# Value products of prompt attention: four key blocks at a time instead of two, with nine exponential buffers instead of six

## The chip, the core and the metric

One NeuronCore of a Trainium2 chip runs the whole program. The time is device microseconds (us) of one execution; the median of three runs is compared. In the profile PE is TensorE (matmuls), PEld its weight loads, DVE is VectorE, ACT is ScalarE, POOL is GpSimd and SP the engine that issues most DMAs.

## What is computed

One inference step of a decoder layer, for a prompt of 1024 tokens and for 8 single tokens with a cache of 1024 positions each: RMS norm, one input projection, then two mixers side by side (sparse attention and a gated delta rule), an output projection, a SwiGLU feed-forward part and a last norm. The change lies in the sparse attention of the prompt, which the reference computes for blocks of 128 queries:

```python
p_cmp = masked_softmax(einsum('bqgrd,bngd->bqgrn', qf, ck), m_cmp)      # 63 compressed keys
o_cmp = einsum('bqgrn,bngd->bqgrd', p_cmp, cv)
s_sel = einsum('bqgrd,bgqkld->bqgrkl', qf, kg)                          # selected key blocks
o_sel = einsum('bgqrkl,bgqkld->bqgrd', masked_softmax(s_sel, m_sel), vg)
p_win = masked_softmax(einsum('bqgrd,bsgd->bqgrs', qf, kw), m_win)      # last 512 keys
o_win = einsum('bqgrs,bsgd->bqgrd', p_win, vw)
return g[..., 0:1] * o_cmp + g[..., 1:2] * o_sel + g[..., 2:3] * o_win
```

There are 8 query heads in 2 groups of 4, each head 64 wide, and one key/value head for a group. All is float32.

## The kernel before, in words

A *unit* is one block of 128 queries (i = 0 to 7) with one head group (g = 0 or 1), 16 in all, in the order of UNITS (L911): i = 2, 1, 0, 5, 4, 3, 7, 6, both groups of each. For a unit the scores are computed twice. `score_maxima` (L1014) puts queries on partitions and finds each row's maximum (DVE, L1049) and sum of exponentials (ACT, L1051), in banks of PSUM named S (three of them); its products are L1044 and L1045. `offset_rows` (L1056) turns them into one additive offset per query and branch, which also holds the gate and the softmax's denominator, and writes it into rows of the tile qo. `values_unit` (L1111) then computes the scores again with keys on partitions: for each block of keys two products (L1131, L1132) into one of two banks named X, an exponential on ACT into a buffer PF (L1134), which is the weighted probability at once, and on some blocks a mask on DVE (L1137). With the offset in place the outputs of the three branches can simply be added up, so all value products of a unit (`weighted`, L1124) accumulate into one bank, O.

A unit's blocks are numbered n = 0 to N-1: n = 0 is the block of 63 compressed keys (64 rows), then come i + 1 blocks of 128 selected keys and up to 5 of the window. N is 3, 5, 7, 9, 11, 12, 13, 14 for i = 0 to 7, so 74 blocks per group and 148 in all. A value product has 64 output columns, half of TensorE's width: an even n writes partitions 0 to 63 of O, an odd one 64 to 127, and `write_unit` (L1151) adds the halves and stores them. The list `late` holds blocks whose value product is not yet issued. Whenever it holds four, the two oldest are taken out and issued, the odd one first; at the unit's end the rest follows in pairs, each after a `yield`. `keep_in_program_order` pins a product behind the PE instruction that was issued before it in the program.

Several streams of work share the engines. `schedule` (L134) interleaves them by a virtual clock: each generator yields its cost and a pause, and the first of the streams whose pause is over goes on. The streams are the rest of the input projection, `small_streams` (L884), and for attention one each for queries, maxima, offsets, values and `attention_post`. small_streams goes through the delta rule, then the attention of the 8 single tokens (`sample_attention`, which gathers cached keys by indirect DMAs into gx, L1309, copies them by DMA into cpx and kx, L1314 and L1315, and multiplies by `compress`, L812), the residual (L1480), and the output projection of the first two thirds of the tokens (`out_proj`, L1530, six matmuls between two yields). Within what the streams put out, the program's builder orders each engine's instructions again by its own estimate of when their data is there.

The steps below are at L1122 to L1126 (`weighted`), L1133 (the buffers), L1138 (when products are due) and L1143 to L1147 (the unit's end).

Of the kernel before, what the change touches and what calls it, by code (L numbers as in the profile page):

```python
# [9 lines left out]
F32 = mybir.dt.float32  # L10
# [74 lines left out]
def hybrid_step(ctx, tc, A, O):  # L85
# [37 lines left out]
    def bank(tag="mm"):  # L123
        tag = ALIAS.get(tag, tag) if tag not in ps_bufs else tag
        if tag == "g":
            return psg.tile([128, 512], F32, name="g", bufs=2)
        return ps_now[0].tile([128, 512], F32, name=tag, bufs=ps_bufs[tag])
# [806 lines left out]
    def attention_values(start, done):  # L934
        for u, (i, g) in enumerate(UNITS):
            yield lambda: done["F"] > u and done["P"] >= u - 0
            start["o", u] = yield from values_unit(start["aw"], start["stack", g], start[u], g, i, start["keep"])
            done["C"] += 1
# [71 lines left out]
    def window(i):  # L1010
        w0 = 128 * max(0, i - 4)
        return 128 * (i + 1), w0, 128 * (i + 1) - w0
# [98 lines left out]
    def values_unit(aw, st, q, g, i, keep):  # L1111
        nk, w0, nw_ = window(i)
        md, mw, mc = keep[:, 0:128], keep[:, 128:256], keep[:64, 256 + 128 * i:384 + 128 * i]
        qt, qo = q
        blocks = [(0, "c", 0, 64, mc)]
        blocks += [(1, "s", 128 * k, 128, md if k == i else None) for k in range(i + 1)]
        blocks += [(2, "w", 128 * k, 128, md if k == i else mw if k == i - 4 else None)
                   for k in range(w0 // 128, i + 1)]
        O = bank("O")
        last = len(blocks) - 1  # L1120

        def weighted(due):  # L1122
            for n, pf, v, w in reversed(due):
                x = mm(O[64 * (n % 2):64 * (n % 2) + 64], lhsT=v, rhs=pf[:w], start=n < 2, stop=n > last - 2)  # L1124
                if n != due[-1][0]:
                    tc.keep_in_program_order(x)  # L1126

        late = []
        for n, (br, nm, a, w, mask) in enumerate(blocks):
            p = bank("X")  # L1130
            mm(p[:w], lhsT=st[nm + "h"][:, a:a + w], rhs=qt, start=True, stop=False)  # L1131
            mm(p[:w], lhsT=st[nm + "l"][:, a:a + w], rhs=qo, start=False, stop=True)  # L1132
            pf = aw.tile([128, 512], F32, name="PF", bufs=6)  # L1133
            S.activation(pf[:w], p[:w], AF.Exp)  # L1134
            if mask is not None:
                pv = pf[:w].rearrange("p (h t) -> p h t", h=4)
                V.tensor_tensor(pv, pv, mask[:, None, :].to_broadcast([w, 4, 128]), op=OP.min)  # L1137
            due = late[:2] if len(late) == 4 else []  # L1138
            del late[:len(due)]
            weighted(due)  # L1140
            late.append((n, pf, st[nm + "v"][:w, a // 128], w))
            yield 0.43 + 0.43 * len(due), 0.4 * (n < 3)
        while late:  # L1143
            due = late[:2]
            del late[:2]
            yield 0.0, 0.5
            weighted(due)  # L1147
        yield 0.87, 1.0
        return O
# [502 lines left out]
    def pair_tiles(gw, ht, u, slots=range(7)):  # L1652
        if u % 2 == 0:
            return [gw.tile([128, 2, 512], F32R, name=f"q{x}") for x in slots]
        a = ht.tile([128, 4, 2, 512], F32R, name="hTa")
        b = ht.tile([128, 3, 2, 512], F32R, name="hTb")
        return [a[:, x] for x in range(4)] + [b[:, x] for x in range(3)]
# [85 lines left out]
    def pair_blocks(raws):  # L1743
        return [r[:, :, 128 * x:128 * x + 128] for x in range(2) for r in raws]
# [253 lines left out]
    with tail, pool("hn") as hp, pool("gw") as gw:  # L1998
# [3 lines left out]
        with pool("psc", space=PSUM) as ps:  # L2002
# [93 lines left out]
            w, a = pair_tiles(gw, None, 0, range(4)), pair_blocks(raws)  # L2096
# [11 lines left out]
        with pool("psd", space=PSUM) as ps:  # L2108
# [11 lines left out]
            for u in range(20):  # L2120
# [17 lines left out]
                w = w_next  # L2138
            keep.flush()
        with pool("psf", space=PSUM) as ps:  # L2140
# [4 lines left out]
            for v in range(20):  # L2145
# [36 lines left out]
                w = w_next  # L2182
# [29 lines left out]
```

## Time and profile before

| | |
|---|---|
| median of three runs | 1788.6 us (1788.4 to 1796.88) |
| the profiled execution | 1790.07 us |
| its span, first to last instruction | 1788.4 us |
| PE busy | 1689.1 us, 94% of the span |
| DVE, ACT, POOL busy | 1123.1, 832.6, 400.5 us |
| first and last start of an L1124 record | 546.9 and 1033.6 us |

Busy time is the union of an engine's instructions, not their sum, and a matmul's record reaches to its modelled end, so consecutive matmuls overlap in the records: what one costs is read from start to start. A product in float32 has two records. In the timeline view, consecutive records of the same form are put in one row, with their count.

### The profile page before, as it was taken

What the parts mean: (1) busy time and instruction counts of PE and PEld (TensorE: products, weight loads), DVE (VectorE), ACT (ScalarE), POOL (GpSimd) and SP (SyncE); (2) the same over time, 40 slices, a digit from 0 to 9 for tenths busy, and PEclk for the clock granted to TensorE, in tenths of its full rate; (3) what the DMA queues carried; (4) which work ended last, traced back from release to release, by engine and by line L of the source; (5) the groups of instructions that cost most, each with busy time, mean ns of one, the idle gap of its engine ahead of it and who ended that gap; (6) DMA issues with size and microseconds to landing.
All of it is one profiled execution on the core that took longest, in us unless ns stands there. A gap on an engine that the chain in (4) does not pass through costs nothing.

```text
span 1788.4 us, 32029 instructions
## 1 busy us (share of the span) xinstructions
PE 1689.1 (94%) x11985; PEld 1502.5 (84%) x11985; DVE 1123.1 (63%) x2841; ACT 832.6 (47%) x1986; POOL 400.5 (22%) x405
## 2 busy tenths in 40 slices
PE   7999989989989989989999989999999999999998
PEld 7999989989876465555567769999999999999997
DVE  6458874588468766656754377544444444868786
ACT  5567742222356656646864454433333333633222
POOL 1214330222112221110023453332332334100000
PEclk9999999999989889899999999999999999999999
DMA  7135444665331475552444342233222323533212
GB/s 237 41 103 193 177 157 132 213 214 178 103 103 36 129 211 143 161 158 75 148 117 138 117 134 63 97 102 111 84 84 83 97 82 108 178 126 124 96 59 95
DMA packets 247584, 223.81 MB, mean 125 GB/s; under 512 B 76121, under 2 KB 226145, under 8 KB 245246
## 3 DMA queue, kind: packets, MB, share of 16 engines
q1 hardware_dynamic: 232404, 188.79, 34.2%
q0 software_dynamic: 7152, 22.43, 3.9%
q10 hardware_dynamic: 7874, 10.56, 1.8%
q8 instruction: 94, 1.54, 0.3%
q14 instruction: 60, 0.49, 0.1%
HBM read 149.08 MB, written 60.40 MB: 117 GB/s over the span
## 4 chain that ended last, share of the span: by engine, by line
PE 58%; DVE 4%; DMA 4%; ACT 4%; issue 2%; POOL 1%; SPq 0%; POOLq 0%; ACTq 0%; DVEq 0%
PE X L1763 13%; PE Z L1937 6%; PE V L1763 6%; PE Z L1919 5%; PE O L1124 4%; PE g L1530 4%; PE Y L1763 3%; PE mm L1455 2%; DMA gx<-in_cache_nsa_kv_dram,ix 2%; PE S L1044 2%; PE X L1131 2%; PE S L1045 1%; PE Y L1979 1%; PE X L371 1%; PE X L1132 1%
## 5 line engine op out<-in xcount | busy, mean ns | idle before, releaser
L77 DVE TENSOR_TENSOR q<-q,q 128x256 fp32r<-128x256 f32 (+5 forms) x234 | 139.2, 610 | 50.5 <-ACT q L77 49.0
L77 ACT CAST q<-q 128x256 fp32r<-128x256 f32 (+2 forms) x195 | 90.3, 495 | 129.2 <-DVE q L77 79.2
L1051 ACT ACTIVATE S<-S,nb 128x512 f32<-128x512 f32 (+4 forms) x256 | 119.8, 469 | 47.3 <-DVE nb L1049 39.9
L1049 DVE TENSOR_REDUCE nb<-S 128x1 f32<-128x512 f32 (+4 forms) x154 | 96.2, 636 | 14.7 <-PE S L1045 13.3
L1134 ACT ACTIVATE PF<-X 128x512 f32<-128x512 f32 (+1 forms) x148 | 84.9, 595 | 43.6 <-PE X L1132 38.0
L287 PE MATMUL X<-xh,ch_h 128*128 128x344 f32 x288 | 95.0, 330 | 0.0
L371 PE MATMUL X<-wh,xh 128*128 128x320 f32 (+1 forms) x288 | 93.6, 325 | 0.0
L77 DVE TENSOR_TENSOR q<-q,Y 128x258 f32<-128x258 f32 x40 | 16.9, 424 | 121.4 <-PE Y L1763 85.2
L77 ACT COPY q<-X 128x258 f32<-128x258 f32 x80 | 30.0, 375 | 135.5 <-PE X L1763 135.5
L287 PE MATMUL X<-xl,ch_h 128*128 128x344 f32 x288 | 92.7, 322 | 0.0
L287 PE MATMUL X<-xh,ch_l 128*128 128x344 f32 x288 | 92.7, 323 | 0.0
L371 PE MATMUL X<-wh,xl 128*128 128x320 f32 (+1 forms) x288 | 91.3, 317 | 0.1
L371 PE MATMUL X<-wl,xh 128*128 128x320 f32 (+1 forms) x288 | 91.2, 317 | 0.1
L1722 POOL TENSOR_TENSOR q<-q,q 128x512 f32<-128x512 f32 x40 | 58.8, 1470 | 135.2 <-DVE q L77 107.4
L1497 POOL TENSOR_TENSOR wol<-woraw,woh 128x1024 fp32r<-128x1024 f32 x18 | 43.7, 2434 | 88.5 <-ACT woh L1496 88.5
L1137 DVE TENSOR_TENSOR PF<-PF,keep 128x512 f32<-128x512 f32 (+1 forms) x56 | 40.3, 725 | 30.5 <-ACT PF L1134 30.2
L77 POOL TENSOR_TENSOR q<-q,q 128x258 f32<-128x258 f32 (+1 forms) x44 | 46.5, 1068 | 48.9 <-DVE q L77 48.9
L1124 PE MATMUL O<-PF,vs 128*64 128x512 f32 x144 | 54.5, 647 | 1.5 <-DVE o L1155 1.5
L287 PEld LDWEIGHTS X<-xh,ch_h 128*128 128x128 f32 x288 | 54.9, 191 | 0.2 <-ACT craw L245 0.2
L252 DVE SCALAR_TENSOR_TENSOR cacc<-craw,stt,cacc 128x1024 f32<-128x1024 f32 x36 | 53.1, 1475 | 3.0 <-ACT cacc L250 2.7
L287 PEld LDWEIGHTS X<-xl,ch_h 128*128 128x128 f32 x288 | 54.8, 190 | 0.1
L371 PEld LDWEIGHTS X<-wl,xh 128*128 128x128 f32 x288 | 54.4, 189 | 0.4 <-DVE wl L350 0.4
(758 smaller groups left out, 5582.6 us busy)
## 6 DMA issues: line engine op xcount, KB each, us to landing
q<-in_w_gate_up_dram SPq DMA_DIRECT2D x40, 512.0 KB
woraw<-in_w_out_dram SPq DMA_DIRECT2D x23, 512.0 KB
q<-g_scr SPq DMA_DIRECT2D x22, 516.0 KB
q<-in_w_down_dram SPq DMA_DIRECT2D x22, 512.0 KB
g_scr<-q SPq DMA_DIRECT2D x40, 258.0 KB
k_scr<-pack SPq DMA_DIRECT2D x8, 1280.0 KB
packr<-k_scr SPq DMA_DIRECT2D x8, 1280.0 KB
cpx<-gx SPq DMA_DIRECT2D x64, 128.0 KB
```

Source lines behind the costliest of these rows:

```text
L77: i = op(*args, **kw)
L287: mm(p[:, :CH], lhsT=a[:, k], rhs=b[:, k, CH * c:CH * c + CH], start=k == 0 and j == 0, stop=k == 7 and j == 2)
L371: mm(p[:, :ncol], lhsT=a[:, k, c0:c0 + 128], rhs=b[k][:, :ncol], start=k == 0 and j == 0, stop=k == 7 and j == 2)
L1049: V.tensor_reduce(out=nb[:, y, br, h0:h0 + per], in_=pv, op=OP.max, axis=AX.X, negate=True)
L1051: S.activation(pv[:, h], pv[:, h], AF.Exp, bias=nb[:, y, br, h0 + h:h0 + h + 1], accum_out=sm[:, y, br, h0 + h:h0 + h + 1])
L1124: x = mm(O[64 * (n % 2):64 * (n % 2) + 64], lhsT=v, rhs=pf[:w], start=n < 2, stop=n > last - 2)
L1134: S.activation(pf[:w], p[:w], AF.Exp)
L1530: mm(p[:, :n], lhsT=x[:, k], rhs=y[:, :n], start=i == 0 and j == 0, stop=i == 7 and j == 2)
L1722: plan.setdefault(step, []).append(lambda: eng.tensor_tensor(out, x, y, op=op))
L1763: mm(p, lhsT=w[n][:, x, c], rhs=y[:, k, 258 * q:258 * q + 258], start=new and k == 0 and j == 0, stop=k == nk - 1 and j == 2, skip_group_c ...
L1919: mm(p[:, q], lhsT=w[2 * x + k2][:, y, c], rhs=b[:, k, 258 * q:258 * q + 258], start=k2 == 0 and k == 0 and j == 0, stop=k2 == 1 and k == ...
L1937: mm(p[:, q], lhsT=w[n][:, x, c], rhs=y[:, k, 258 * q:258 * q + 258], start=new and k == 0 and j == 0, stop=k == 1 and j == 2, skip_group_ ...
```

## The change

The buffers PF become nine. Value products are issued when `late` holds six blocks, and then the four oldest; the rest at a unit's end goes in groups of four as well. Within a group the order is pair by pair, the odd block of each first: 1, 0, 3, 2. All but the first of a group are pinned. The cost that the stream reports grows with the group.

```diff
         def weighted(due):
-            for n, pf, v, w in reversed(due):
+            order = [d for k in range(0, len(due), 2) for d in due[k:k + 2][::-1]]
+            for n, pf, v, w in order:
                 x = mm(O[64 * (n % 2):64 * (n % 2) + 64], lhsT=v, rhs=pf[:w], start=n < 2, stop=n > last - 2)
-                if n != due[-1][0]:
+                if n != order[0][0]:
                     tc.keep_in_program_order(x)
...
-            pf = aw.tile([128, 512], F32, name="PF", bufs=6)
+            pf = aw.tile([128, 512], F32, name="PF", bufs=9)
...
-            due = late[:2] if len(late) == 4 else []
+            due = late[:4] if len(late) == 6 else []
             del late[:len(due)]
             weighted(due)
...
         while late:
-            due = late[:2]
-            del late[:2]
+            due = late[:4]
+            del late[:4]
             yield 0.0, 0.5
             weighted(due)
```

## Rows read from the trace of the kernel before

**Rows 1.** The head of the page: span, and PE's and PEld's busy time.

```profile
span 1788.4 us, 32029 instructions
PE 1689.1 (94%) x11985; PEld 1502.5 (84%) x11985; DVE 1123.1 (63%) x2841; ACT 832.6 (47%) x1986; POOL 400.5 (22%) x405
```

**Rows 2.** Windows view of the attention stage: stretch, length, then busy time of each engine.

```profile
620.00:690.00 70.00, 58.63 (x335) 40.42 (x334) 46.88 (x131) 45.57 (x140) 14.70 (x21) 0.93 0.73 206
...
740.00:800.00 60.00, 51.59 (x277) 32.56 (x279) 36.73 (x102) 34.86 (x91) 10.63 (x17) 0.94 0.65 179
800.00:1035.00 235.00, 222.99 (x1212) 150.80 (x1209) 127.31 (x305) 140.53 (x346) 53.81 (x37) 0.98 0.37 116
```

**Rows 3.** The same windows for L1124 alone: PE busy, PEld busy.

```profile
547.00:620.00 73.00, 24.58 (x52) 4.33 (x52) 0.93 0.31 83
...
800.00:1035.00 235.00, 51.59 (x158) 9.44 (x154) 0.98 0.37 116
sum 488.00, PE 109.20 PEld 19.79; mean PE 21.84 PEld 3.96
```

**Rows 4.** Chain of waits by line, in 620 to 690, 740 to 800, 800 to 1035 us.

```profile
by line: DMA gx<-in_cache_nsa_kv_dram,ix 21.5%; DMA kx<-gx 18.9%; PE O L1124 7.0%; SPq L1314 6.9%; issue 6.5%; PE S L1044 4.7%; PE S L1045 4.0%; PE g L835 3.9%; DVE nb L1049 3.7%; ACT kt L838 3.1%; ACT S L1051 3.0%; PE g L1330 2.6%; PE g L1
...
by line: DMA gx<-in_cache_nsa_kv_dram,ix 35.3%; DMA kx<-gx 11.6%; issue 6.5%; PE O L1124 5.9%; PE X L1131 5.8%; DVE nb L1049 5.1%; PE X L1132 4.2%; PE g L1321 3.0%; PE g L835 2.9%; DVE S L1048 2.6%; PE S L1044 2.0%; DVE PF L1137 2.0%; DVE o
...
by line: PE g L1530 29.1%; PE O L1124 16.6%; PE X L1131 6.4%; PE X L1132 5.8%; ACT S L1051 5.7%; PE S L1044 5.6%; PE S L1045 4.3%; issue 3.2%; PE g L812 3.0%; POOL wol L1497 2.1%; PE g L1480 1.8%; PE g L1436 1.3%; PE g L1346 1.3%; ACT woh L
```

**Rows 5.** The tile PF's view: exponentials, count, shortest, median, longest in ns.

```profile
L1134 ACT ACTIVATE PF<-X x148: 569/597/647, 543.9 to 1030.5; 128x512 f32<-128x512 f32 x132, 64x512 f32<-64x512 f32 x16
```

**Rows 6.** PE's timeline (start, duration, line): first and last stretch of L1124.

```profile
546.93 1.07 PE L1124 MATMUL O<-PF,vs 128*64 128x512 f32 x2
...
1029.95 1.94 PE L1124 MATMUL O<-PF,vw 128*64 128x512 f32 x8
```

**Rows 7.** PE's timeline around one pair by itself.

```profile
1026.23 0.39 PE L1131 MATMUL X<-qt_a,kwh 128*128 128x512 f32 x1
1026.46 0.39 PE L1132 MATMUL X<-qo,kwl 128*128 128x512 f32 x1
1026.78 1.08 PE L1124 MATMUL O<-PF,vs 128*64 128x512 f32 x4
1027.79 0.45 PE L1530 MATMUL g<-mh,woh 128*128 128x384 f32 x1
1028.07 0.34 PE L1530 MATMUL g<-ml,woh 128*128 128x384 f32 x1
1028.25 0.33 PE L1530 MATMUL g<-mh,wol 128*128 128x384 f32 x1
```

**Rows 8.** PE's timeline where two pairs of equal form run on.

```profile
552.43 1.08 PE L1124 MATMUL O<-PF,vs 128*64 128x512 f32 x4
553.34 1.03 PE L1124 MATMUL O<-PF,vw 128*64 128x512 f32 x4
554.30 0.38 PE L1044 MATMUL S<-kwh,qt_a 128*128 128x256 f32 x1
```

**Rows 9.** PE's timeline where blocks 1 and 0 and a pair run on.

```profile
837.78 1.07 PE L1124 MATMUL O<-PF,vs 128*64 128x512 f32 x2
838.78 1.07 PE L1124 MATMUL O<-PF,cvn 64*64 64x512 f32 x2
839.78 1.08 PE L1124 MATMUL O<-PF,vs 128*64 128x512 f32 x4
840.79 0.50 PE L1131 MATMUL X<-qt_a,kwh 128*128 128x512 f32 x1
```

**Rows 10.** Waits of PE and of ACT, 547 to 1035 us: total, times, longest.

```profile
PE X L1131 <- ACT PF L1134: 2.8, 4, 1.5
...
ACT PF L1134 <- PE X L1132: 35.4, 33, 2.9
...
ACT PF L1134 <- PE O L1124: 5.0, 2, 4.3
```

## The prediction

> **What bounds the kernel now.** I read the head of the page first: TensorE (PE) is busy for 94% of the span [rows 1], so only what shortens PE's queue, or a wait in it, can shorten the kernel much. The change touches one stage, prompt attention, whose value products (L1124) run from 546.93 to some 1034 us. So I split that stage, 547 to 1035 us, with the windows view. It is not one regime. Between 800 and 1035 us PE is busy for 223.0 of 235 us; between 620 and 690, and between 740 and 800, for only 58.6 of 70 and 51.6 of 60 [rows 2]. The same windows for L1124 alone give 109.2 us in all, of which 24.6 + 51.6 = 76.2 us, 70%, lie before 620 and after 800 us [rows 3]. Then the chain of waits of the stretches: in 620 to 690 and 740 to 800 its largest item is the gather of cached keys (gx), 21.5% and 35.3%; from 800 us on it is PE's lines L1530 and L1124 [rows 4]. So PE time saved before 620 or after 800 us should be time saved; in between, most of it becomes a longer wait for a gather.
>
> **What a value product costs.** One L1124 product has 64 output columns, half of the array, and a pair takes both halves. The records come two to a product. The 148 exponentials [rows 5] mean 148 products. In the timeline of PE I count 81 stretches of L1124 without another line between; the first and the last stand in [rows 6]. A pair by itself: four products' records in 1.01 us, from 1026.78 to 1027.79. Around it PE loses more: the score product before it starts 0.32 us ahead of the pair, where score products follow each other at 0.23 us, and the first L1530 after it holds its place for 0.28 us where the next one takes 0.18 [rows 7]. That is 0.09 + 0.10 = 0.19 us for going in and out. Two pairs in a row (552.43 to 554.30) take 1.87 us, not 2 x 1.01 = 2.02: the second one is 0.15 us cheaper [rows 8]. One pair is different: block 0, the compressed keys, has 64 rows, its form is 64*64, and it does not run beside block 1: block 1 takes 1.00 us, block 0 another 1.00, and the pair behind it 1.01 [rows 9]. A pair appended to block 0 thus saves the way in and out, and nothing inside.
>
> **The change part by part.** *Clusters.* By the code a unit of N blocks gave ceil(N/2) groups before, 80 over the 16 units, and gives 22 x 2 = 44 after (N = 3, 5, 7, 9, 11, 12, 13, 14 give 1, 2, 2, 3, 3, 3, 4, 4). No product is added or removed. The 81 stretches should become 44: 37 x 0.19 = 7.0 us of PE. Of the 36 new junctions 16 follow block 0 and save nothing inside; 20 join products of the same form, and 4 of these already stand in one stretch in the timeline, so 16 x 0.15 = 2.4 us more. Sum: 9.4 us of PE time.
>
> Against the second term stands a rule of the Trainium skill, TensorE: Matmul & The Clock Gate, section The mechanism: weight loads overlap running matmuls only where the row groups differ; all products of a cluster but block 0 share theirs, so by the rule a second pair would wait for its loads. The trace disagrees with it here, since the second pair of [rows 8] is the cheaper one; by the rule the PE sum would be the first term alone, 7.0 us.
>
> *Later emission.* Products are held until six blocks wait, not four. The newest block of a cluster is three blocks old when it is issued, as that of a pair was, so its exponential and mask are as long done; I cost it at nothing. Where that cover is thin is a unit's end: with N = 12 the rest is four blocks with the last, masked one among them, pinned behind the others. PE would then stand for part of one exponential, 0.60 us [rows 5], twice in the kernel: bounds 0 and 1.2 us, taken as 0 because the two products ahead of it run 1.01 us. The last unit (N = 13) ends in four products and one in both versions.
>
> *Nine buffers.* ScalarE waited for a value product to free an exponential's buffer twice, 5.0 us in all [rows 10]. Six held blocks would fill six buffers; with nine, the block that reuses a buffer comes three blocks after the cluster that frees it, where it came two blocks after the pair. So these waits may go: bounds 0 and 5.0 us. I take 0, since ScalarE's time is not on the chain there, and keep 5.0 for the good end. The three extra buffers move the addresses of what shares the pool; no row shows what that costs. I bound it by the longest such wait, up to 5.0 us either way, and take 0, because tiles of the next stage wait for the attention's end in either case.
>
> *Queues.* No DMA is added. A unit's store can come about one pair later on ScalarE's queue; the loads of it are far behind except in the last unit, whose end is unchanged.
>
> *The sum.* 9.4 us of PE, of which the 70% that lie before 620 and after 800 us shorten the kernel: 6.6 us. The profiled execution took 1790.07 us, 1788.4 of it the span [rows 1], so it would be 1783.5; it lies 1.5 us above the median of the three runs, so against that median I predict 1788.6 - 6.6 = 1782.0 us. Half a per cent, 8.9 us, is about what a measurement of this kernel can tell from no change; the forecast lies inside it.
>
> **The rivals.** *More comes through.* The gather stretches shrink as well, because PE also gets through its other work sooner there, and the buffer waits go: 9.4 + up to 5.0 us, 1779 to 1774. For it speaks that L1124 is on the chain even in 620 to 690 us (7.0%) [rows 4]; against it that gathers pace these stretches.
>
> *The clusters do not form.* The program's order is the builder's, not the source's alone: it may put other products between those pinned. For it: block 1 and block 0, a pair in the source, stand apart in six of sixteen units in PE's timeline. Against: of the pairs of equal form only one is broken. Time: 1788.6, with a few us either way.
>
> *ScalarE becomes the bound, and the kernel slower.* Place: the eight score products ahead of a cluster. They need two banks (X), each free again after its exponential of 0.60 us [rows 5]; two products take 2 x 0.23 = 0.46 us [rows 7]. Four blocks want 4 x 0.60 = 2.4 us of ScalarE and give it 1.84 us of PE; in the old rhythm two blocks wanted 1.2 us and had a pair's 1.01 us besides. If nothing stands between the scores, PE waits 0.27 (the third and fourth block start when the first two exponentials end, without any latency) to 0.54 us (the whole difference) per four blocks, 37 times: 10 to 20 us, less the 6.6: 1792 to 1802. It decides where no other stream's products fall between the scores. Against it: PE waits for ScalarE's exponentials at L1131 only 2.8 us now, while ScalarE waits 35.4 us for score products [rows 10]: ScalarE has the slack. Also, the interleaving of streams puts an L1530 piece into every third or fourth block's place, since four blocks and a cluster count as long as two pairs did. Half of it would only eat the gain.
>
> **How the numbers follow.** The forecast, a gain of 4 to 9 us or a little more: 0.42, of which 0.07 beyond 8.9 us. More comes through: 0.27, all faster. Clusters not formed: 0.10, the same. ScalarE's wait: 0.21, of which 0.08 only eats the gain and 0.13 is slower by over 0.5%. So faster 0.27 + 0.07 = 0.34; the same 0.35 + 0.10 + 0.08 = 0.53; slower 0.13. The forecast's own range is 1779 to 1785. The range asked for leaves out a tenth at each end: below, the good rival with both terms and the addresses' luck, 1772; above, the lower part of ScalarE's wait, 1794.
>
> **What would show it.** Right: L1124 in some 44 to 50 stretches; two pairs of equal form in 1.87 us and block 1, block 0 and a pair in 3.01; L1124's busy time hardly changed, since overlapped records count once, but the stage 547 to 1035 us shorter by 5 to 9 us, mostly after 800 us; the gather stretches about as long as before. Wrong: over 60 stretches (the builder pulled them apart); PE's wait at L1131 for exponentials at 10 us or more in place of 2.8; a stage that shrinks by over 10 us, which would mean that the gathers follow PE; or a change before 547 us or in the feed-forward stages, which would be the moved addresses.

## The result, and the profile after

The changed kernel takes **1802.45 us** (median of 4 runs, 1802.15 to 1802.6) against 1789.26 us for the kernel before (4 runs, 1788.4 to 1796.88): ratio 1.0062, interval 1.004 to 1.0083. It is 13 us slower. The forecast was 6.6 us faster, and the result lies above the range. A second series of the same changed kernel gave 1.0069 (experiment 9).

From the value products on, line numbers are one higher than before: the value product is L1125, the scores L1132 and L1133, the projection L1531. The head of the page and the windows of the stage answer to [rows 1, 2]; columns as there, the granted clock third from the end:

```profile
span 1800.6 us, 32005 instructions
PE 1695.3 (94%) x11985; PEld 1508.5 (84%) x11985; DVE 1120.8 (62%) x2841; ACT 833.6 (46%) x1986; POOL 400.0 (22%) x405
```

```profile
620.00:690.00 70.00, 59.60 (x315) 40.84 (x315) 43.61 (x124) 42.61 (x129) 13.78 (x20) 0.85 0.69 190
...
740.00:800.00 60.00, 54.59 (x280) 33.88 (x281) 34.11 (x102) 33.13 (x89) 13.14 (x20) 0.86 0.69 188
800.00:1035.00 235.00, 222.71 (x1201) 147.84 (x1200) 129.71 (x325) 144.64 (x357) 46.76 (x36) 0.99 0.37 115
```

From 800 us on PE's busy time and its number of records are nearly the same. In the first gather stretch PE gets through fewer records (315, before 335), and in both the granted clock is lower (0.85 and 0.86, before 0.93 and 0.94). For L1125 alone, against [rows 3], nothing was saved: 111.1 us of busy time, before 109.2.

```profile
547.00:620.00 73.00, 22.05 (x48) 4.10 (x48) 0.95 0.28 72
...
800.00:1035.00 235.00, 54.90 (x166) 10.56 (x164) 0.99 0.37 115
sum 488.00, PE 111.13 PEld 20.76; mean PE 22.23 PEld 4.15
```

**The clusters did not form.** In PE's timeline I count 76 stretches of value products, not 44. The timeline of one unit of 14 blocks shows why:

```profile
896.24 1.08 PE L1125 MATMUL O<-PF,vs 128*64 128x512 f32 x4
897.25 0.50 PE L1132 MATMUL X<-qt_a,ksh 128*128 128x512 f32 x1
...
898.07 0.40 PE L1133 MATMUL X<-qo,ksl 128*128 128x512 f32 x1
898.39 1.08 PE L1125 MATMUL O<-PF,vs 128*64 128x512 f32 x4
899.40 0.50 PE L1132 MATMUL X<-qt_a,kwh 128*128 128x512 f32 x1
...
900.83 0.47 PE L1133 MATMUL X<-qo,kwl 128*128 128x512 f32 x1
901.22 1.08 PE L1125 MATMUL O<-PF,vs 128*64 128x512 f32 x4
```

One pair, two blocks of scores, the next pair: the old rhythm. The first product of a group is pinned to nothing and the others only come after it, so the builder is free to put each pair forward; as I read it, to where its own estimate has the exponentials ready.

**Where the time went.** The last value product starts at 1029.4 us in place of 1033.6, 4 us sooner. But the projection ends 12.5 us later, alone on PE: after the last value product 66 of its 384 matmuls are left, where the kernel before had none. Of the timeline of PE, the first and the last of them, and what follows:

```profile
1028.91 1.07 PE L1125 MATMUL O<-PF,vw 128*64 128x512 f32 x2 [0.18 <-DVE PF L1138]
1029.92 0.44 PE L1531 MATMUL g<-mh,woh 128*128 128x384 f32 x1
...
1041.29 0.34 PE L1531 MATMUL g<-mh,wol 128*128 128x384 f32 x1
1041.47 0.83 PE L1582 MATMUL Y<-K,rn 128*128 128x128 f32 x6
1046.49 1.44 PE L1568 MATMUL g<-K,sqo 128*128 128x1 f32 x6 [4.19 <-DVE sqo L1563]
1050.48 1.22 PE L1582 MATMUL Y<-K,rn 128*128 128x128 f32 x4 [2.55 <-DVE rn L1573]
```

A statistic of the projected rows (sqo) then comes late, and PE stands twice, 6.7 us. From the end of both streams to the last matmul of the last third's projection (`out_part`) I read 41.8 us in place of 35.8; I call this the handover. It is counted from the later of the two streams. Counted from the end of the projection, that last matmul comes 40.9 us later before and 41.9 in the changed kernel: so here the next stage follows the projection, which ends late because it starts late. (In runs 13, 15 and 18 below, where the value products end more than 20 us after the projection, that matmul comes 31.5 to 31.6 us after them.) Here are the first of its three kinds of matmul, first and last start; before, changed kernel, and run 17 of the experiments below (each row one kernel):

```profile
L1530 PE MATMUL g<-mh,woh x128: 331/334/522, 911.0 to 1028.4; 128*128 128x384 f32 x128
```

```profile
L1531 PE MATMUL g<-mh,woh x128: 331/334/522, 922.8 to 1040.9; 128*128 128x384 f32 x128
```

```profile
L1532 PE MATMUL g<-mh,woh x128: 332/334/522, 910.0 to 1029.9; 128*128 128x384 f32 x128
```

The projection takes as long as before. In its stream it comes behind the attention of the single tokens, whose gathers (gx) the chain of [rows 4] had named. The view of that tile has POOL's issue of the 32 gathers, first and last start, for the same three kernels:

```profile
L1309 POOL DMA_INDIRECT gx<-in_cache_nsa_kv_dram,ix x32: 933/940/1234, 603.8 to 788.1; - x32
```

```profile
L1310 POOL DMA_INDIRECT gx<-in_cache_nsa_kv_dram,ix x32: 932/942/1384, 603.9 to 798.1; - x32
```

```profile
L1311 POOL DMA_INDIRECT gx<-in_cache_nsa_kv_dram,ix x32: 932/942/1359, 603.2 to 789.6; - x32
```

Same start, last gather 10 us later in the changed kernel. What held them back at first shows in POOL's timeline at the beginning. First the kernel before, then the changed one:

```profile
605.18 0.98 POOL L1309 DMA_INDIRECT gx<-in_cache_nsa_kv_dram,ix  x1 [0.30 <-issue]
606.50 0.52 POOL L998 MEMSET qo<- 64x512 f32 x1 [0.35 <-PE X L1132]
607.08 0.10 POOL L1020 MEMSET sm<- 128x4 f32 x1
613.25 0.52 POOL L998 MEMSET qo<- 64x512 f32 x1 [6.07 <-PE X L1132]
614.90 0.15 POOL L1061 MEMSET off<- 128x64 f32 x1 [1.12 <-PE S L1105]
615.82 0.94 POOL L1309 DMA_INDIRECT gx<-in_cache_nsa_kv_dram,ix  x1 [0.78 <-DVE qo L1106]
617.07 0.93 POOL L1309 DMA_INDIRECT gx<-in_cache_nsa_kv_dram,ix  x1 [0.30 <-issue]
```

```profile
605.24 1.38 POOL L1310 DMA_INDIRECT gx<-in_cache_nsa_kv_dram,ix  x1 [0.30 <-issue]
610.32 0.52 POOL L998 MEMSET qo<- 64x512 f32 x1 [3.69 <-PE X L1133]
610.89 0.10 POOL L1020 MEMSET sm<- 128x4 f32 x1
618.06 0.52 POOL L998 MEMSET qo<- 64x512 f32 x1 [7.07 <-PE X L1133]
618.99 0.94 POOL L1310 DMA_INDIRECT gx<-in_cache_nsa_kv_dram,ix  x1 [0.41 <-DVE o L1156]
623.97 0.15 POOL L1061 MEMSET off<- 128x64 f32 x1 [4.04 <-PE S L1105]
624.88 0.94 POOL L1310 DMA_INDIRECT gx<-in_cache_nsa_kv_dram,ix  x1 [0.77 <-DVE S L1048]
```

POOL issues the gathers, and it also clears tiles of the attention streams. A memset of qo waits for the last score product of an earlier unit (L1133); a memset of off waits for an offset's transposition (L1105). Whatever stands behind them on POOL waits too. In the changed kernel the third gather stands behind a memset that is released at 618.06 in place of 613.25, and the memset of off now stands between the third gather and the fourth: that one goes out at 624.88 in place of 617.07. The two buffers that these gathers fill were not what they waited for, as far as the trace shows: the copies out of the first two gathers had been issued by 613.56 us, and VectorE's own (vb) ended at 616.79. Against the kernel before the gathers are 6 us late by the seventh and 10 us late by the last.

Two readings limit this. PE doesn't stand longer for it: from the first value product to the end of both streams it is idle for 37.0 of 487.3 us before and for 37.5 of 490.8 in the changed kernel, so other streams' matmuls fill the waits, and what comes late is one stream. And not all of the 12.2 us between the two spans (1800.6 and 1788.4) arises in the attention: its first score product (L1044) already starts at 518.6 us in place of 515.7. In run 11, where only the projection's pause differs from the kernel before, it starts at 520.2, so executions differ by that much there anyhow.

The wait of PE for exponentials went from 2.8 us [rows 10] to 3.7 us; the buffer wait of ScalarE (5.0 us, [rows 10]) is gone from the list:

```profile
ACT PF L1135 <- PE X L1133: 39.1, 34, 3.8
...
PE X L1132 <- ACT PF L1135: 3.7, 6, 1.4
```

### The profile page after: what moved, and what is told of

Its sections match the earlier page's. It is cut to its first block, busy times and chain, and to the rows that moved or that the text cites. A ratio compares the mean times of both kernels' runs of the same rounds, so it can differ in the third digit from the quotient of the medians.

```text
span 1800.6 us, 32005 instructions
## 1 busy us (share of the span) xinstructions
PE 1695.3 (94%) x11985; PEld 1508.5 (84%) x11985; DVE 1120.8 (62%) x2841; ACT 833.6 (46%) x1986; POOL 400.0 (22%) x405
## 4 chain that ended last, share of the span: by engine, by line
PE 58%; DVE 5%; DMA 4%; ACT 3%; issue 2%; POOL 1%; SPq 0%; POOLq 0%; ACTq 0%; DVEq 0%
PE X L1764 12%; PE Z L1938 6%; PE V L1764 6%; PE Z L1920 5%; PE O L1125 5%; PE g L1531 3%; PE Y L1764 3%; PE mm L1456 2%; PE S L1044 2%; DMA gx<-in_cache_nsa_kv_dram,ix 2%; PE X L1132 2%; PE S L1045 2%; PE X L1133 1%; PE Y L1980 1%; PE X L371 1%
## 5 line engine op out<-in xcount | busy, mean ns | idle before, releaser
L1051 ACT ACTIVATE S<-S,nb 128x64 f32<-128x64 f32 (+4 forms) x256 | 120.0, 470 | 41.8 <-DVE nb L1049 32.1
L1135 ACT ACTIVATE PF<-X 128x512 f32<-128x512 f32 (+1 forms) x148 | 85.4, 596 | 42.4 <-PE X L1133 39.1
L1125 PE MATMUL O<-PF,vs 128*64 128x512 f32 x144 | 55.6, 660 | 2.3 <-DVE PF L1138 1.9
L287 PEld LDWEIGHTS X<-xh,ch_l 128*128 128x128 f32 x288 | 54.9, 191 | 0.0
```

Source lines behind the costliest of these rows:

```text
L287: mm(p[:, :CH], lhsT=a[:, k], rhs=b[:, k, CH * c:CH * c + CH], start=k == 0 and j == 0, stop=k == 7 and j == 2)
L1051: S.activation(pv[:, h], pv[:, h], AF.Exp, bias=nb[:, y, br, h0 + h:h0 + h + 1], accum_out=sm[:, y, br, h0 + h:h0 + h + 1])
```

## The experiments

Medians are given with the kernel before in the same series. "Stretches" are those of value products in PE's timeline of the profiled execution (81 before, 76 in the changed kernel); "left" is the number of projection matmuls that start behind the last value product there; "gathers" is the time from the first to the last issue of gx in the profiled execution (184.3 us before, 194.2 in the changed kernel). OGAP is the pause of the projection's stream after each turn (L508: 0.9).

| | edit | median, before, us | ratio | stretches | left | gathers |
|---|---|---|---|---|---|---|
| 1 | before, 9 buffers | 1793.65, 1792.59 | 1.0013 (0.9995 to 1.003) | 82 | 0 | 186.3 |
| 2 | before, 9 buffers, pairs at six | 1788.69, 1792.59 | 0.9975 (0.9959 to 0.9991) | 80 | 0 | 181.4 |
| 3 | 2 again | 1788.03, 1792.19 | 0.9983 (0.9966 to 1.0) | 80 | 0 | 180.2 |
| 4 | before, 11 buffers, pairs at eight | 1795.08, 1792.51 | 1.001 (0.9991 to 1.0029) | 75 | 0 | 183.9 |
| 5 | after, all products pinned | 1848.58, 1792.59 | 1.0327 (1.0299 to 1.0355) | 54 | 66 | 190.6 |
| 6 | before, all products pinned | 1843.37, 1792.59 | 1.0291 (1.0258 to 1.0325) | 74 | 0 | 177.4 |
| 7 | after, OGAP 0.8, groups tied | 1804.8, 1792.51 | 1.008 (1.0054 to 1.0105) | 64 | 0 | 189.9 |
| 8 | before, pairs tied | 1798.67, 1792.19 | 1.0041 (1.0025 to 1.0057) | 80 | 0 | 186.8 |
| 9 | after, unchanged | 1804.31, 1791.26 | 1.0069 (1.0043 to 1.0095) | 76 | 66 | 194.3 |
| 10 | after, OGAP 0.8 | 1798.0, 1791.26 | 1.0033 (1.0013 to 1.0052) | 75 | 0 | 190.1 |
| 11 | before, OGAP 1.3 | 1794.89, 1791.26 | 1.0016 (0.9999 to 1.0033) | 79 | 84 | 184.0 |
| 12 | after, unit's rest in pairs | 1797.79, 1791.26 | 1.0034 (1.0017 to 1.005) | 77 | 12 | 186.9 |
| 13 | 12, OGAP 0.85 | 1798.51, 1792.51 | 1.004 (1.0021 to 1.0059) | 81 | 0 | 188.6 |
| 14 | before, rest in fours, OGAP 0.7 | 1792.0, 1792.51 | 1.0006 (0.999 to 1.0022) | 81 | 0 | 187.1 |
| 15 | after, OGAP 0.85, pay spread | 1792.83, 1792.71 | 0.9997 (0.9982 to 1.0013) | 78 | 0 | 187.5 |
| 16 | before, OGAP 0.85, pay in lumps | 1795.45, 1792.71 | 1.0022 (1.0011 to 1.0033) | 77 | 0 | 187.3 |
| 17 | after, pay spread | 1790.91, 1792.03 | 0.999 (0.998 to 1.0) | 77 | 6 | 186.4 |
| 18 | 10, pay spread | 1792.84, 1792.03 | 1.0001 (0.9989 to 1.0013) | 78 | 0 | 185.2 |

The gathers' time alone does not rank the runs: runs 12 and 16, with 186.9 and 187.3 us, are at 1.0034 and 1.0022, runs 14 and 15, with 187.1 and 187.5 us, at 1.0006 and 0.9997. That late gathers cost time is read from the order of one stream in the traces; no run changes them alone.

**Runs 1 to 4: the parts of the change that are not groups.**

```diff
-            pf = aw.tile([128, 512], F32, name="PF", bufs=6)
+            pf = aw.tile([128, 512], F32, name="PF", bufs=9)
```

> The kernel before with nine exponential buffers and nothing else. Theory A (the way the work is emitted, not the buffers, moved the streams against each other): 1789 us, within 3 us. Theory B (the three extra buffers alone, by their addresses and by letting exponentials run further ahead, cost the 13 us): 1798 to 1803 us. The builder puts L1124 in 82 stretches here, 81 before.

```diff
-            pf = aw.tile([128, 512], F32, name="PF", bufs=6)
+            pf = aw.tile([128, 512], F32, name="PF", bufs=9)
...
-            due = late[:2] if len(late) == 4 else []
+            due = late[:2] if len(late) == 6 else []
```

> Pairs as before, from nine buffers, but only once six blocks wait: the change's later emission without its groups of four. Theory A (emission that is two blocks later lengthens each unit in the streams' virtual clock and costs the time): 1796 to 1803 us, with the output projection ending some 10 us after the last value product. Theory C (it is the groups of four that cost, as bursts on PE): 1789 us, within 3 us. 80 stretches.

> The kernel before with nine buffers and its pairs held until six blocks wait, once more, unchanged from the earlier run of it (0.9975). If holding the pairs back is worth something by itself, the ratio is again 0.996 to 0.999. If that run was luck of its chip, it is 1.000 to 1.002, as with pairs held until eight wait (1.001).

The same with `bufs=11` and `len(late) == 8`:

> Pairs, issued only once eight blocks wait, from eleven buffers: one step further than the run with six blocks, which was 4 us faster than the kernel before. If room between an exponential and its product is worth time: 3 to 6 us below the kernel before. If that gain came from the order that the builder happened to make: anywhere within 5 us of it.

Neither the addresses of three more buffers nor the later emission is the loss. Pairs held until six wait gain 3 to 4.5 us by the ratios, in two series; held until eight they gain nothing. So more room alone does not help, and I put the gain down to the order that results, which no run isolates. Runs 2 and 3 are the fastest version found.

**Runs 5 to 8: making the groups form.** In 5 and 6 all value products are pinned behind the PE instruction before them in the program:

```diff
-                if n != order[0][0]:
-                    tc.keep_in_program_order(x)
+                tc.keep_in_program_order(x)
```

> The changed kernel with the first product of each group pinned as well, so that the groups of four do form: the builder puts them in 54 stretches instead of 76. Theory A (the groups are cheap where they form, and the loss is elsewhere): 22 x 0.19 us and up to 20 x 0.15 us less than the changed kernel, 7 us of PE, 70% of it in the end: 1796 to 1799 us. Theory C (a cluster that holds PE starves ScalarE and the other streams): 1805 us or more, with PE's wait for exponentials at L1131 at 10 us or more.

> The kernel before with the first product of each pair pinned as well: nothing else moves, pairs aren't taken ahead by the builder; 74 stretches instead of 81. Theory A: 7 x 0.19 = 1.3 us less at most, 1786 to 1790 us. A rival (it is the freedom to take products ahead that fills PE's waits, and a pin takes that away): 1795 us or more.

Both came out some 50 us above what I expected, with groups of four or of two alike. They lie in the open ranges of the rivals (1805 us or more, 1795 or more), but the sign of the first, 10 us or more of PE waiting for exponentials, reads 8.0 us in run 5. Where a group stands behind a `yield`, as the rest of a unit does, the instruction before its first product can belong to another stream, and the pin ties the value stream to it. In run 5's view of waits new ones stand on top; 12.8 us for the residual's load, which belongs to another stream:

```profile
PE g L1321 <- DMA kx<-gx: 12.9, 9, 6.8
PE g L1480 <- DMA xr<-xraw: 12.8, 3, 5.6
```

So runs 5 and 6 say nothing of groups: the pin costs as much with pairs. A narrower tie puts the first product behind the last score product of its own stream, which is passed in as `score`:

```diff
-        def weighted(due):
+        def weighted(due, score):
...
+                else:
+                    tc.add_manual_dep(x.ins, score.ins.name, mybir.DependencyInfo(
+                        mybir.DependencyClass.NoSync, mybir.DependencyReason.DATA), reason="behind its scores")
```

> The changed kernel with the pause at 0.8 and with the first product of each group tied behind the score product that it follows in its own stream, not behind whatever PE issued last: 64 stretches as against 75 in the run with the pause alone. If merged stretches are worth what the rows of before say: 11 x 0.19 and some 8 x 0.15 us of PE, 3 us, less than that run. Theory C (bursts hold up the other streams): 3 us or more above it.

> The kernel before with one thing added: the first product of each pair is tied behind the score product that its own stream issued last (an order on TensorE's queue, no wait for data). 80 stretches of value products in the builder's order, as before, and nothing of the projection left behind the last one. If the tie itself was what made the tied changed kernel (1804.8) 6.8 us slower than the untied one with the same pace (1798.0), this one should be slower than the kernel before by as much, 1.003 to 1.004 or more. If it was the clusters of four, which formed more often there (64 stretches in place of 75), this one should be within 3 us of the kernel before, 0.998 to 1.002, with TensorE's waits in the stage near the 36 us of the kernel before.

Run 7 alone looked as if formed groups were what costs: 64 stretches, and 6.8 us more than run 10 with 75. Run 8 took that away: the tie costs 6.5 us without any group of four. With the tie, groups of four cost 6.1 us more than pairs (1804.8 and 1798.67); without it, run 10 costs 6.7 us more than its kernel before. So the price is about the same whether 64 or 75 stretches stand, and standing together is not the loss. Whether it gains anything these runs can't tell: the 3 us that were expected of 11 stretches fewer are less than the width of their intervals. Where a group did form, two pairs cost what they did in [rows 8]: 1.87 us, from 743.27 to 745.14; this is PE's timeline in run 7, where the scores are L1135:

```profile
743.27 1.08 PE L1125 MATMUL O<-PF,vs 128*64 128x512 f32 x4
...
745.14 0.50 PE L1135 MATMUL X<-qt_a,kwh 128*128 128x512 f32 x1
```

**Runs 9 to 11: the end of the stage.** OGAP is set to 0.8 in the changed kernel and to 1.3 in the kernel before.

> The changed kernel once more, beside the others of this call. It was 13.2 us above the kernel before on the first chip. If that holds: 1799 to 1806 us, or 1.004 to 1.008 of the kernel before in this call.

> The changed kernel with the output projection's pause in the virtual clock at 0.8 instead of 0.9, so that no projection matmul is left after the last value product (66 in the changed kernel, none before), with 75 stretches as against 76. Theory D (the units became cheaper in the virtual clock, the projection got too few turns and ends alone, and its statistics then stand open at the handover to the next stage): 5 to 8 us less than the changed kernel in this call, with the handover, from the end of both streams to the last matmul of L1546, at 36 us instead of 41.8. Theory C (bursts inside the stage): no change, within 3 us.

> The kernel before with that pause at 1.3 instead of 0.9: 84 projection matmuls are left after the last value product, and no other line is touched. Theory D: 5 to 9 us more than the kernel before, with the handover at 41 to 43 us. If the end doesn't matter: within 3 us of the kernel before.

With the shorter pause nothing of the projection is left over; the handover is 36.9 us, and 6.3 us come back. That looks like half the loss. But in run 11 the kernel before is given the same kind of end (84 left, handover 40.8 us), and it loses 3.6 us with an interval that reaches below 1. In its profiled execution the stage, from the first value product to the end of both streams, is 482.5 us long in place of 487.2, which makes up for the longer handover. And run 17 below has a handover of 40.8 us and loses nothing. A long handover is no loss by itself; what counts is when the two streams end, and the projection's end is set by its start as well as by its pace.

**Runs 12 to 14: which groups.** Fours in the loop and pairs for the rest, then with a balanced end; then pairs in the loop and one group for the rest:

```diff
         while late:
-            due = late[:4]
-            del late[:4]
+            due = late[:2]
+            del late[:2]
```

> The changed kernel with the rest of a unit issued in pairs again, each after its pause; groups of four only in the main loop. 12 projection matmuls are left after the last value product. Theory D: most of the end's cost is gone, 4 to 7 us less than the changed kernel. Theory C: no change within 3 us, since the groups of four in the main loop stay.

> Groups of four in the main loop only, the rest of a unit in pairs, and the projection's pause at 0.85, so that no projection matmul is left after the last value product (12 in the run without that). Theory D: against that run 4 to 7 us less, so 1.000 to 1.002 of the kernel before; handover 34 to 37 us. Theory F (groups of four in the main loop cost inside the stage): still 5 us or more above the kernel before, with a balanced end.

> The other half alone: pairs from six buffers in the main loop, and only the rest of a unit in one group of up to four; the projection's pause is 0.7, which leaves no projection matmul at the end. Theory D: within 3 us of the kernel before. Theory G (the one group at a unit's end, without the pause between two pairs, costs inside the stage): 5 us or more above it.

With OGAP 0.85 and none left, 13 has a handover of 31.6 us, 4 shorter than the kernel before, and is still 6 us slower; 14 costs nothing. The loss that stays with a balanced end belongs to the loop's groups; their nine buffers and later emission cost nothing in runs 1 to 4. What is left are two things: the products, and the `yield` behind them.

**Runs 15 to 18: what the stream pays.** The loop ends in `yield 0.43 + 0.43 * len(due), ...` (L1142), the value stream's price in the virtual clock. With pairs it pays 0.43 and 1.29 by turns, with fours 0.43 three times and then 2.15. Runs 15, 17 and 18 keep the groups and the total of a unit, and spread it over the blocks from the fourth on, so that the pay also starts three blocks sooner than the first lump:

```diff
-            yield 0.43 + 0.43 * len(due), 0.4 * (n < 3)
+            paid = 4 * max(0, (len(blocks) - 3) // 4)
+            yield 0.43 + 0.43 * (3 <= n < 3 + paid), 0.4 * (n < 3)
```

Run 16 keeps the pairs and pays in lumps:

```diff
-        late = []
+        late, owed = [], 0
...
+            owed = 0 if n < 4 else owed + len(due)
+            pay = owed if n % 4 == 2 or n >= len(blocks) - 2 else 0
+            owed -= pay
-            yield 0.43 + 0.43 * len(due), 0.4 * (n < 3)
+            yield 0.43 + 0.43 * pay, 0.4 * (n < 3)
```

> The changed kernel with its groups of four, OGAP 0.85 and one more thing changed: what the stream pays for its value products is spread, 0.43 more on each block from the fourth on, where a group of four paid for all its products at once (2.15 in one turn). The total per unit is the same; nothing of the projection is left behind the last value product. If the groups' lumpy pay, and with it the turns of the other streams, is what costs 6 us inside the stage of the balanced kernels with groups of four (1.0033 and 1.004), this one should be at 0.999 to 1.0015. If the groups of four themselves cost it, it should stay at 1.0025 to 1.005.

> The kernel before with its pairs and six buffers as they are, but paid for in lumps: what two pairs cost is paid in one turn, every fourth block (0.43, 0.43, 0.43, 2.15), with OGAP 0.85 so that nothing of the projection is left behind the last value product. If the lumpy pay costs the 6 us, this one should be at 1.0025 to 1.005, without any group of four. If the groups of four themselves cost it, it should be within 0.999 to 1.0015.

> The changed kernel with the spread pay as its only difference (OGAP 0.9 as it was): 6 matmuls of the projection are left behind the last value product in the builder's order, where the changed kernel has 66. If the changed kernel's whole loss lies in how the streams take turns (the projection left over at the end, and the lumps of pay), this one should be at 0.999 to 1.002. If the groups of four or the nine buffers cost something themselves, it should be at 1.003 or more.

> The kernel with groups of four and OGAP 0.8 (1.0033) with the spread pay as its only difference. If the lumps were what cost it 6 us, it should be at 0.998 to 1.0015. If the result with OGAP 0.85 (0.9997) was a lucky order of the builder, it should be at 1.0025 to 1.005.

Run 17 is the changed kernel with this one line altered, and all of the loss is gone: 0.999. Run 18 is run 10 with the line altered: 1.0033 becomes 1.0001, intervals just meeting at 1.0013. Run 15 agrees. Run 16 points the same way from the other side, more weakly: 2.7 us by the medians and 0.2% by the ratio, between what was expected if the lumps cost it (4.5 us or more) and if they do not. It also has the shorter pause, and no run has that pause with the kernel before as it was. In run 17 PE's timeline ends the stage with the last value products, six projection matmuls, and the next stage at once:

```profile
1026.50 2.79 PE L1125 MATMUL O<-PF,vw 128*64 128x512 f32 x10
1029.23 0.44 PE L1532 MATMUL g<-mh,woh 128*128 128x384 f32 x1
...
1030.23 0.34 PE L1532 MATMUL g<-mh,wol 128*128 128x384 f32 x1
1030.40 0.83 PE L1583 MATMUL Y<-K,rn 128*128 128x128 f32 x6
```

Its third and fourth gather stand together again on POOL:

```profile
613.17 0.52 POOL L998 MEMSET qo<- 64x512 f32 x1 [4.93 <-PE X L1133]
614.10 0.94 POOL L1311 DMA_INDIRECT gx<-in_cache_nsa_kv_dram,ix  x1 [0.41 <-DVE nb L1049]
615.35 0.94 POOL L1311 DMA_INDIRECT gx<-in_cache_nsa_kv_dram,ix  x1 [0.30 <-issue]
617.75 0.15 POOL L1061 MEMSET off<- 128x64 f32 x1 [1.47 <-PE S L1105]
```

And the projection starts at 910.0 us, where it starts at 922.8 in the changed kernel (rows above), and ends at 1030.6. So its late end goes with its late start, and not with the time from its first matmul to its last, 118 to 121 us in all three kernels.

How lumps do it can be read in `schedule`, though no run isolates it: a stream whose pause of 0.9 is over gets one turn, after a lump of 2.15 as after 0.9, so what a lump pays beyond a pause buys the others nothing. That the pay of run 17 is more even and that it starts sooner are not told apart. The smaller total (by the code 80 products are paid in the loops of the 16 units where it was 96) is not the cause, since run 17 pays the same 80. Nor can the builder's luck with one order well be, since the spread pay came out without loss at three settings of the pause. How exactly one lump turned into the order on POOL was not followed through the builder.

## Why the prediction was wrong

**"The 81 stretches should become 44: 37 x 0.19 = 7.0 us of PE."** This step failed first. 76 stretches stand, so most of the 9.4 us never arose; L1125's busy time even rose by 1.9 us. I held against the rival "the clusters do not form" that of the pairs of equal form only one was broken. But pairs say little of fours: the exponentials of two neighbouring blocks are done soon after each other, those of four are spread further, and the builder, as I read it, uses that. The rival, at 0.10, had the mechanism right and the time (1788.6) wrong. The price inside a cluster, 1.87 us, was right where it applied, so the trace disagrees here too with the sentence of the Trainium skill that weight loads overlap running matmuls only where the row groups differ (TensorE: Matmul & The Clock Gate, section The mechanism). The same section also lets a load into the background weight buffer be pulled ahead, which the prediction left out. The price was just hardly used.

**"Four blocks and a cluster count as long as two pairs did."** This sentence, put against a rival, is the step behind the 13 us. I read `yield` as a price that stays in sum and took its turns for neutral. They are not: the same groups with the same sum, paid in lumps, are at 1.0069 and, paid evenly, at 0.999 (run 9 against run 17).

**"Queues. No DMA is added. ... the gather stretches about as long as before."** No DMA was added, but POOL's queue was reordered: the third gather came behind a memset released 5 us later and the fourth behind one that had stood ahead of both, and the last issue came 10 us later. The projection, in the same stream, started 12 us later. That this path is how the lumps cost their 13 us is argued from the traces, not isolated. The chain had told me that gathers pace 620 to 690 and 740 to 800 us, and that should have led to the question what stands ahead of them on POOL.

**"6.6 us, of which the 70% ..."** was not put to a test, since nothing was saved; run 17 has the groups without the loss, but 77 stretches, so no run shows what clusters that form would be worth.

**Later emission and nine buffers, at 0:** right as terms (runs 1 and 4 within the measurement), and the 5 us bound on the addresses held in run 1 (1 us by the medians, 5.4 us at the interval's upper end). That the order of run 2 gains 3 to 4.5 us was outside what I had costed.

**The last unit, "whose end is unchanged":** its products are, but the stage no longer ended with it; the projection did.

**The slower rival, ScalarE,** gave 1792 to 1802, close to the number and for the wrong reason: its own sign, 10 us or more of PE waiting for exponentials, shows 3.7 us.

**The test that I set** (over 60 stretches, and gather stretches that change) did show that the clusters did not form; it could not show why time was lost. The sign for moved addresses, a change before 547 us, reads 2.9 us at the first score product, but run 11, with six buffers, shows 4.5.

## What to carry to other kernels

Where streams are interleaved by a cost that each one reports, the size of a single report is a part of the schedule: a change of grouping should keep the pay as evenly spread as it was, and be timed once with the new grouping and the old pay, and once the other way round. Before you cost a moved step at nothing, list what stands ahead of the pacing transfers on the queue that issues them, however idle that engine is (POOL was 22% busy here). And a pin gives an order, not a neighbourhood: look at the builder's order before you count what a cluster saves. Last, a PE that is as busy as before can hide a loss: look for the stream that the next stage waits for, here the projection, and for what starts it late.

## What the runs showed of the hardware

The run time of this kernel went with the clock that it was granted. Over the 134 runs of the kernel before that were taken beside the experiments, a mean granted clock lower by 0.001 went with 0.75 us more. The changed kernel had 0.9706 on average over 8 runs, the kernel before 0.9746: by an estimate from these numbers some 3 of the 13 us go with the clock, and no run tells whether as an effect of the waits or beside them. Run 8, at 0.9758, is 6.5 us slower without a lower clock. From 1041 to 1052 us PE was busy for 4.3 of 11 us, and the granted clock of that window was 0.72, between the two levels of 1.2 and 2.4 GHz; a window view of the changed kernel:

```profile
1041.00:1052.00 11.00, 4.26 (x23) 3.98 (x22) 5.66 (x19) 2.29 (x4) 3.19 (x2) 0.72 0.82 235
```

Reordering without any work added or removed moved this kernel by some 4 us one way (runs 2 and 3, with three more buffers) and by 6 us the other (run 8). A predicted gain of 6 us on PE is no larger than that.
